# Operands of the second phase from memory, inner P7 in its last block, and the inner weights of P2 formed one phase earlier

## The chip, the cores and the metric

The kernel runs on one core of one Trainium2 chip. The metric is the device time of one execution in microseconds (us), for the kernel before as the median of three runs. A profile is taken of one execution. Its engines are PE (matmuls), DVE and ACT (elementwise work, copies out of PSUM), POOL and SP (which issue most of the DMAs).

## The reference

With one layer of the pooling mixer the computation is, for 4096 frames of width 1024 in float32:

```python
u, gate = jnp.split(rms_norm(x, norm_w) @ in_w, 2, axis=-1)      # 1024 -> 2 x 1024
ug = u.reshape(b, s, POOL_GROUPS, POOL_GROUP_DIM)                # 4 groups of 256
pooled = stack([trailing_mean(ug[:, :, g], w) for g, w in enumerate((2, 4, 8, 16))]) - ug
mixed = jnp.einsum('bsgc,gcd->bsgd', pooled, group_w) + group_b
y = mixed.reshape(b, s, POOL_WIDTH) * scale * jax.nn.silu(gate)
h = x + y @ out_w
return rms_norm(h, final_norm_w)
```

The linear map of each group commutes with the trailing mean, so the kernel folds `group_w` into the left half of `in_w` beforehand and pools afterwards.

## The kernel before

All large products are done by a Strassen-Winograd scheme: a product of 2 x 2 blocks takes seven block products, P1 to P7, of sums and differences of the blocks. Every float32 operand is split into a high part (a copy on ACT, rounded to fp32r) and a low part (a subtraction on DVE), and each block product is three passes of fp32r matmuls (high x high, high x low, low x high). `split(dst, src)` issues the copy and the subtraction.

There are three phases. Phase a is one half of the input projection, phase b the other half, each over four blocks of 1024 frames; phase o is the output projection over eight blocks of 512 frames. Each block is seven steps, one per product: P1, P2, P7, P6, P5, P4, P3 in phases a and b, and P1, P7, P6, P2, P5, P4, P3 in phase o. A plain step of phases a and b is 48 matmuls of 512 columns. In some steps a product is itself done by a further level of the scheme, in seven products of quarter size ("inner" products): P7 of blocks 1 and 2 of phase b (`product_seven`, 84 matmuls of 256 columns, with copies of partial sums from bank to bank on ACT, here called moves), P2 from block 1 of phase o on (`product_inner`, `add_inner`), and an own P7 from block 2 of phase o on. Inner products need inner weights, which are differences of quarters of the plain weights, again split in two.

The names that the rest uses:

- `op0` to `op3` (`op_85` to `op_88` in lists of instructions) are the four buffers of split operands that PE reads; `st` and `vt` are pools of eleven and eight buffers of 512 KB, `w` the split weights, `bank0` to `bank7` (`bank_69` to `bank_76`) the PSUM banks. In lists of instructions each buffer has a number (`st_89` to `st_99` and higher for `st`, `vt_100` to `vt_107` for `vt`).
- `load_in`, `form_in`, `split_in` load, form and split the operands of a step of phases a and b, some steps ahead. In phase a the normalized blocks and one difference are also stored by POOL (`sd`: P1, P2, P7 and P4), phase b loads those and forms the sums for P6, P5 and P3 again.
- `evict_in` copies the banks out after a step: SiLU of the gates after P1 and P2 (into two buffers taken from the pools), and so on. `pool` makes the trailing means of a finished block: for each of its two tiles a short sum, a scan, one scaled difference and two scaled adds on DVE, and then SP stores the tile to `yd` and its buffer goes back to the pool. `pool_due(n)` calls it for what has become due at step n.
- A buffer that comes back to its pool can be taken at once; the instruction that writes it next waits for whatever still reads it, a store included. `take` and `take_v` give out the buffer that has been free longest.
- `load_inner`, `sum_inner`, `split_weight` (L865 and before) load, form and split inner weights in phase o. `load_w(wod, i)`, `form_wb`, `split_wb` bring the output weights in during block 3 of phase b.

The instructions of each engine are put in order by a scheduler when the program is built; `tc.issue_after(x)` holds what is issued inside it behind the instruction x. At run time each engine works its list off in order.

```python
        elif i == P2:
            ev["11"] = [take() for _ in range(2)]
            for c, u in enumerate(cells(ev["11"])):
                last = copy(halved(u), plain(ps[c]), AF.Silu)
```

## Time and profile before

| | |
|---|---|
| median of three runs | 907.35 us (906.75 to 907.79) |
| the profiled execution | 907.23 us |
| its span, first to last instruction | 905.4 us |
| mean granted PE clock | 0.998 |
| PE busy | 895.8 us, 4518 matmuls |
| DVE, ACT, POOL busy | 757.0, 517.5, 118.5 us |
| phase b, blocks 0 to 3 start at about | 323, 396, 468 and 540 us |
| phase o starts at about | 613 us |

In the rows of the profile a line of the timeline gives the start (us), the time from the first start to the last end of the merged instructions, the engine, the line of the kernel, the operation, output<-input by name, the shapes, the count, and in brackets how long the engine had been idle and which work ended that. L79 is the helper through which every instruction of DVE, ACT, POOL and SP is recorded, so these are told apart by names and shapes. L807 are plain products, L753 the inner P7 of phase b, L949 the inner products of phase o, L1681 a few matmuls at the very start. Matmuls are pipelined: a merged row ends some 0.16 us after the next matmul could start.

### The profile page before, as it was taken

The numbers are of one execution on the slowest core, as the hardware profiler recorded it, in microseconds if no ns is written. First come the engines' busy times: TensorE is split into PE (matmuls) and PEld (weight loads), VectorE is DVE, ScalarE is ACT, GpSimd is POOL, SyncE is SP. The second block draws the span as 40 slices with busy tenths as digits, with TensorE's granted clock in tenths as the row PEclk, the third lists the DMA queues.
The fourth block names the chain that finished last, engine by engine and source line by source line (L and its number), as shares of the span: only waits on it lengthen the run. The fifth ranks groups of instructions, "written<-read, shape, count | busy, mean of one in ns | idle before, by whom it ended". The sixth has DMA issues, their size and how long they took to land.

```text
span 905.4 us, 12216 instructions
## 1 busy us (share of the span) xinstructions
PE 895.8 (99%) x4518; PEld 791.1 (87%) x4518; DVE 757.0 (84%) x925; ACT 517.5 (57%) x853; POOL 118.5 (13%) x208
## 2 busy tenths in 40 slices
PE   9999999999999999999999999999999999999996
PEld 7888888888888888889889888888889899999995
DVE  3899995985995999797599499599798878888797
ACT  7869547547445565346545636654657466565464
POOL 0020100100110000000000000001133333343330
PEclk9999999999999999999999999999999999999999
DMA  9987767577675453333554474638483865945953
GB/s 343 401 305 226 273 239 241 187 274 233 235 267 198 164 199 103 99 112 111 202 199 135 179 279 143 197 117 239 143 236 88 212 180 147 233 153 131 259 181 116
DMA packets 71692, 180.49 MB, mean 199 GB/s; under 512 B 6608, under 2 KB 24656, under 8 KB 71632
## 3 DMA queue, kind: packets, MB, share of 16 engines
q1 hardware_dynamic: 54976, 132.50, 42.6%
q0 software_dynamic: 15936, 46.16, 17.6%
q10 hardware_dynamic: 720, 1.06, 0.3%
q8 instruction: 35, 0.57, 0.3%
q14 instruction: 25, 0.20, 0.1%
HBM read 118.86 MB, written 60.83 MB: 198 GB/s over the span
## 4 chain that ended last, share of the span: by engine, by line
PE 87%; DVE 5%; ACT 3%; DMA 2%; issue 2%; POOL 0%; SPq 0%; DVEq 0%; ACTq 0%; POOLq 0%
PE bank L807 78%; PE bank L949 5%; DVE vt L79 2%; PE bank L753 2%; DVE op L79 2%; DMA st<-yd 1%; PE bank L447 1%; DVE st L79 1%; ACT op L79 1%; DMA early<-in_wut 1%; ACT st L79 1%; ACT w L79 0%; ACT vt L79 0%; DMA st<-wod 0%; DVE w L79 0%
## 5 line engine op out<-in xcount | busy, mean ns | idle before, releaser
L807 PE MATMUL bank<-op,w 128*128 128x512 f32 x2592 | 560.9, 379 | 0.1
L807 PEld LDWEIGHTS bank<-op,w 128*128 128x128 f32 x2592 | 489.4, 189 | 70.3 <-ACT vt L79 0.5
L807 PE MATMUL bank<-w,op 128*128 128x512 f32 (+1 forms) x1044 | 230.5, 377 | 0.0
L807 PEld LDWEIGHTS bank<-w,op 128*128 128x128 f32 x1044 | 192.3, 189 | 25.0
L79 DVE TENSOR_TENSOR op<-st,op 128x1024 fp32r<-128x1024 f32 x116 | 141.0, 1222 | 49.7 <-ACT op L79 49.3
L79 ACT ACTIVATE op<-st 128x1024 fp32r<-128x1024 f32 x116 | 121.4, 1051 | 68.7 <-PE bank L807 27.6
L79 ACT ACTIVATE op<-vt 128x1024 fp32r<-128x1024 f32 x67 | 70.4, 1053 | 59.3 <-DVE vt L79 38.7
L79 ACT ACTIVATE vt<-bank 128x512 f32<-128x512 f32 (+1 forms) x124 | 69.6, 580 | 48.0 <-PE bank L807 44.2
L79 DVE TENSOR_TENSOR op<-vt,op 128x1024 fp32r<-128x1024 f32 x67 | 80.9, 1221 | 17.5 <-ACT op L79 17.4
L79 DVE TENSOR_TENSOR st<-st,st 128x1024 f32<-128x1024 f32 (+1 forms) x55 | 63.9, 1181 | 17.6 <-ACT st L79 16.8
L79 POOL DMA_DIRECT2D vt<-in_x x26 | 23.3, 937 | 390.7 <-DVE vt L79 353.8
L79 ACT ACTIVATE bank<-bank 128x512 f32<-128x512 f32 (+1 forms) x78 | 38.7, 498 | 43.5 <-PE bank L807 32.1
L79 DVE TENSOR_TENSOR vt<-bank,vt 128x512 f32<-128x512 f32 (+1 forms) x94 | 54.2, 603 | 7.1 <-PE bank L949 4.6
L79 ACT ACTIVATE st<-bank 128x512 f32<-128x512 f32 (+1 forms) x58 | 33.0, 587 | 31.2 <-PE bank L807 17.4
L79 ACT ACTIVATE st<-st 128x1024 f32<-128x1024 f32 x33 | 34.8, 1056 | 22.6 <-DVE st L79 19.6
L79 DVE TENSOR_TENSOR st<-bank,st 128x512 f32<-128x512 f32 (+1 forms) x68 | 41.2, 625 | 7.4 <-PE bank L807 4.1
L79 DVE TENSOR_TENSOR st<-st,vt 128x1024 f32<-128x1024 f32 (+1 forms) x36 | 41.6, 1175 | 2.2 <-DMA vt<-rd 2.2
L949 PEld LDWEIGHTS bank<-w,op 128*128 128x128 f32 x312 | 40.4, 191 | 1.7
L949 PE MATMUL bank<-w,op 128*128 128x256 f32 x312 | 41.1, 275 | 0.0
L79 DVE TENSOR_TENSOR w<-st,w 128x1024 fp32r<-128x1024 f32 (+1 forms) x27 | 31.6, 1182 | 9.3 <-ACT w L79 9.2
L79 DVE TENSOR_TENSOR_SCAN vt<-vt,window 128x1040 f32<-128x1040 f32 x16 | 38.0, 2381 | 0.3 <-DMA yd<-vt 0.3
L79 DVE TENSOR_TENSOR vt<-vt 128x1024 f32<-128x1024 f32 (+3 forms) x42 | 37.6, 898 | 0.1
(115 smaller groups left out, 720.7 us busy)
## 6 DMA issues: line engine op xcount, KB each, us to landing
st<-in_xt SPq DMA_DIRECT2D x28, 512.0 KB, 6.2
sd<-st POOLq DMA_DIRECT2D x28, 512.0 KB, 4.4
st<-sd SPq DMA_DIRECT2D x26, 512.0 KB, 4.5
st<-in_x SPq DMA_DIRECT2D x21, 512.0 KB, 6.3
yd<-st SPq DMA_DIRECT2D x19, 512.0 KB, 2.9
vt<-yd SPq DMA_DIRECT2D x17, 512.0 KB, 10.4
out<-vt POOLq DMA_DIRECT2D x17, 512.0 KB, 3.3
st<-wod SPq DMA_DIRECT2D x16, 512.0 KB, 4.3
```

The costliest lines, as they stand in the source:

```text
L79: r = f(*args, **kwargs)
L447: latest[0] = nc.tensor.matmul(ps, a[:, kk, 2 * j + t, :], maps, start=t + m == 0, stop=t == 1 and m == len(pairs) - 1,).ins
L753: latest[0] = nc.tensor.matmul(cell(n, c).rearrange("p (a s) -> p a s", s=2), x1, x2, start=i == P1 and k + m == 0, stop=k == 1 and m == 2 ...
L807: latest[0] = nc.tensor.matmul(ps, a, b, start=start and n == 0, stop=stop and n == 2, skip_group_check=True).ins
L949: latest[0] = nc.tensor.matmul(ps, x1, x2, start=start and k + n == 0, stop=k == 1 and n == 2, skip_group_check=True,).ins
```

## The change

It does five things.

1. Phase a stores all seven operands of each block (except P6 of block 0), 22 stores of 512 KB more on POOL. Phase b loads them on SP and no longer forms them on DVE. The history of the pooling (16 columns) is copied in phase b by POOL instead of ACT.
2. P7 of block 3 of phase b is also done as an inner product. The plain P7 weight that was kept for it (`load_plain`, `split_plain`) is gone. `pool_due` is held behind the latest split at P2 of that block.
3. The inner weights of P2 are formed in block 3 of phase b: loaded at P2, summed at P6, split and stored as pairs at P5 and P4, and loaded by POOL in block 0 of phase o. The inner weights of P7 take their place in phase o, all in block 1. The output weights come in five steps (P7 to P3) instead of seven, and their splits stand behind the latest eviction.
4. A difference of weights that phase a saves (`save_t3`) is made in two parts.
5. In the last block of phase o `add_inner` stands ahead of the other evictions of P2, the split of P4's operand behind them, and one normalized row moves from step P2 to step P4.

```diff
@@ sd
-            for i in (P1, P2, P7, P4)
+            for i in range(P1, P7 + 1)
+            if (b, i) != (0, P6)
@@ load_in
+        if q and (b or i not in (P6, P4)):
+            s[operand[i]] = load_saved(b, i)
...
@@ inner_in
-        return q == 1 and 0 < b < NB - 1 and i == P7
+        return q == 1 and b > 0 and i == P7
...
@@ split_in
-        if i == P6 and (q or b):
+        if i == P6 and q == 0 and b:
             form_s4(b)
...
@@ save_inner, take_inner (new)
+        for p in ps:
+            place = next_kept()
+            t = st.keep()
+            home = versions(t)
+            latest_copy[0] = copy(home[0], raws[i][p]).ins
+            latest_split[0] = sub(home[1], raws[i][p], home[0].bitcast(F32)).ins
+            gpsimd.dma_start(out=innerd[p], in_=t)
+            give_kept(place)
...
+                t = st.keep()
+                gpsimd.dma_start(out=t, in_=innerd[p])
+                home = versions(t)
...
@@ pool
+            elif q:
+                gpsimd.tensor_copy(out=v[:, :, 0:HIST], in_=tails[:, g])
             else:
                 copy(v[:, :, 0:HIST], tails[:, g])
@@ evict_o
         if inner and i == P2:
             inner["rows"] = [hs[b][0, j][:, 0] for j in range(2)]
+            if final:
+                add_inner(0, (0, 0))
...
@@ steady, P2 of the last block
-            split(ready[P4], s["22"])
-            give(s.pop("22"))
-            if final:
-                norm_row(b - 1, 0, 1)
+            if not final:
+                split(ready[P4], s["22"])
+                give(s.pop("22"))
             InOrder.on = not final
             product_out(P2, ready.pop(P2), sets, False)
             evict_o(b, P2, sets)
+            if final:
+                split(ready[P4], s["22"])
+                give(s.pop("22"))
...
@@ split_reach
-        if kind == "b" and 0 < b < NB - 1 and i == P6:
+        if kind == "b" and b > 0 and i == P6:
...
@@ forming
-        (0, P4): lambda: load_inner(P2),
-        (0, P3): lambda: sum_inner(P2),
-        (1, P1): lambda: split_weight(P2, P7, P6),
...
+        ("b", NB - 1, P2): lambda: load_inner(P2),
+        ("b", NB - 1, P6): lambda: sum_inner(P2),
+        ("b", NB - 1, P5): lambda: save_inner(P2, P7, P6),
+        ("b", NB - 1, P4): lambda: (save_inner(P2, P4, P5), end_weights(P2)),
+        ("o", 0, P5): lambda: take_inner(P2, P5),
+        ("o", 0, P3): lambda: take_inner(P2, P7, P6, P4),
+        ("o", 1, P7): lambda: load_inner(P7),
...
@@ main loop
-        pool_due(n)
+        with tc.issue_after(latest_split[0]) if (kind, b, i) == ("b", NB - 1, P2) else nullcontext():
+            pool_due(n)
...
             if kind == "b" and b == NB - 1:
-                load_w(wod, i)
+                for p in {P1: (), P2: (), P7: (P1,), P6: (P2, P7), P5: (P6, P5)}.get(i, (i,)):
+                    load_w(wod, p)
```

How the lists of the engines move, at three places. The first is DVE in block 3 of phase b, from step P1 into step P7. Before, a low part of an operand (`op`) stands ahead of each tile of pooling (the scan is the SCALAR_TENSOR_TENSOR row with `window`):

```order
L79 TENSOR_TENSOR op_87<-st_3689,op_87 128x1024
L79 SCALAR_TENSOR_TENSOR st_91<-vt_106,colt,st_91 128x512 x2
L79 SCALAR_TENSOR_TENSOR vt_103<-vt_105,window 128x1040
L79 TENSOR_REDUCE window<-vt_100 128x1
L79 SCALAR_TENSOR_TENSOR vt_103<-vt_103,vt_105 128x2x512
L79 TENSOR_REDUCE window<-vt_104 128x1
L79 SCALAR_TENSOR_TENSOR st_93<-vt_103,colt,st_93 128x512 x2
L79 TENSOR_TENSOR op_88<-vt_107,op_88 128x1024
```

In the changed program, in step P2:

```order
L79 TENSOR_TENSOR op_87<-vt_103,op_87 128x1024
L79 TENSOR_REDUCE window<-vt_107 128x1
L79 TENSOR_REDUCE window<-vt_105 128x1
L79 SCALAR_TENSOR_TENSOR vt_100<-vt_107,window 128x1040
L79 SCALAR_TENSOR_TENSOR vt_104<-vt_105,window 128x1040
L79 SCALAR_TENSOR_TENSOR vt_100<-vt_100,vt_107 128x2x512
L79 SCALAR_TENSOR_TENSOR vt_104<-vt_104,vt_105 128x2x512
L79 SCALAR_TENSOR_TENSOR vt_102<-vt_100,colt,vt_102 128x512 x2
L79 SCALAR_TENSOR_TENSOR st_98<-vt_104,colt,st_98 128x512 x2
L79 TENSOR_TENSOR op_88<-st_94,op_88 128x1024
L79 TENSOR_REDUCE window<-vt_100 128x1
L79 TENSOR_TENSOR op_86<-st_95,op_86 128x1024
```

Both tiles of pooling now stand in one piece between the low part of op_87 and those of op_88 and op_86, and the tile in st_98 is the last of them.

The second place is ACT at the end of step P2 of the same block. Before, with the plain P7 to follow, the four evictions of P2 (the first, second, third and fifth row) have these buffers:

```order
L79 ACTIVATE vt_103<-bank_69 128x512
L79 ACTIVATE vt_103<-bank_70 128x512
L79 ACTIVATE st_92<-bank_71 128x512
L79 ACTIVATE w_1_80<-st_90 128x1024
L79 ACTIVATE st_92<-bank_72 128x512
L79 ACTIVATE op_88<-st_91 128x1024
```

In the changed program, with the inner P7 and its moves (`128x256`) behind them:

```order
L79 ACTIVATE vt_101<-bank_69 128x512
L79 ACTIVATE vt_101<-bank_70 128x512
L79 ACTIVATE op_86<-st_95 128x1024
L79 ACTIVATE st_98<-bank_71 128x512
L79 ACTIVATE st_98<-bank_72 128x512
L79 ACTIVATE bank_71<-bank_69 128x256
L79 ACTIVATE st_95<-bank_69 128x256
L79 ACTIVATE bank_72<-bank_70 128x256
L79 ACTIVATE st_95<-bank_70 128x256
```

The third and fourth evictions now go into st_98, the buffer of the last pooled tile above, and the moves that inner P7 needs stand behind them.

The third place is DVE in the last block of phase o, around step P2; `add_inner` is the row that adds a bank in `128x2x128`. Before:

```order
L79 TENSOR_TENSOR op_87<-vt_102,op_87 128x1024
L79 SCALAR_TENSOR_TENSOR vt_104<-vt_104,ors_0_6674,st_89 128x1024
L79 TENSOR_TENSOR vt_103<-bank_71,vt_103 128x512
L79 TENSOR_TENSOR vt_101<-bank_72,vt_101 128x512
L79 TENSOR_TENSOR vt_103<-bank_69,vt_103 128x2x128
L79 TENSOR_TENSOR op_88<-st_90,op_88 128x1024
```

In the changed program:

```order
L79 TENSOR_TENSOR vt_105<-bank_69,vt_105 128x2x128
L79 TENSOR_TENSOR st_95<-bank_72,st_95 128x512
L79 TENSOR_TENSOR vt_105<-bank_71,vt_105 128x512
L79 TENSOR_TENSOR op_86<-vt_107,op_86 128x1024
L79 TENSOR_TENSOR op_87<-st_4261,op_87 128x1024
```

The first addition from `bank_69` stood behind the low part of an operand, a normalized row (the row with `ors`) and two evictions, and stands ahead of them now.

## The prediction

> **What bounds the kernel now.** I read the page's parts 1 and 4 first, then the timelines of TensorE (PE) where it pauses.

> ```profile
> span 905.4 us, 12216 instructions
> PE 895.8 (99%) x4518; PEld 791.1 (87%) x4518; DVE 757.0 (84%) x925; ACT 517.5 (57%) x853; POOL 118.5 (13%) x208
> PE bank L807 78%; PE bank L949 5%; DVE vt L79 2%; PE bank L753 2%; DVE op L79 2%; DMA st<-yd 1%; PE bank L447 1%; DVE st L79 1%; ACT op L79 1%; DMA early<-in_wut 1%; ACT st L79 1%; ACT w L79 0%; ACT vt L79 0%; DMA st<-wod 0%; DVE w L79 0%
> ```

> PE works for 99% of the span. Time is won only by giving PE less to do or by taking away its few pauses, and work taken from DVE, ACT or a queue counts only where PE waits for it. This is PE around inner P7 of block 1 of phase b, and on to inner P7 of block 2:

> ```profile
> 417.32 2.84 PE L753 MATMUL bank<-op,w 128*128 128x256 f32 x24
> 419.99 0.83 PE L753 MATMUL bank<-op,inner 128*128 128x256 f32 x6
> ...
> 426.92 45.27 PE L807 MATMUL bank<-op,w 128*128 128x512 f32 x209
> 489.08 2.84 PE L753 MATMUL bank<-op,w 128*128 128x256 f32 x24
> ```

> The inner product runs from 417.32 to 426.92, 9.60 us. From there to the next one are six plain products, 62.16 us, 10.36 each. After the start-up PE pauses visibly at three places. The first is the start of P7 in block 3 of phase b:

> ```profile
> 559.98 1.79 PE L807 MATMUL bank<-op,w 128*128 128x512 f32 x6
> 559.47 1.06 ACT L79 ACTIVATE w<-st 128x1024 fp32r<-128x1024 f32 x1 [5.88 <-DMA st<-wod]
> 560.44 1.07 ACT L79 ACTIVATE vt<-bank 128x512 f32<-128x512 f32 x2
> ```

> Six matmuls at 0.216 (10.36 over 48) and a last one of 0.38 are 1.46; the row has 1.79, so 0.33 us is a pause. ACT stood 5.88 us waiting for an output weight, and the evictions behind it were late. The other two are in blocks 1 and 7 of phase o, where an inner product waits for a sum that DVE adds from a bank (`add_inner`):

> ```profile
> 668.12 2.75 PE L807 MATMUL bank<-w,op 128*128 128x512 f32 x12
> 671.19 0.94 PE L949 MATMUL bank<-inner,op 128*128 128x256 f32 x6 [0.31 <-DVE vt L79]
> 880.38 4.05 PE L807 MATMUL bank<-w,op 128*128 128x512 f32 x18
> 885.05 0.94 PE L949 MATMUL bank<-inner,op 128*128 128x256 f32 x6 [0.61 <-DVE vt L79]
> ```

> Twelve matmuls from 668.12 give 670.71, so 0.48 until 671.19, and 0.11 more inside (0.94 against 0.83): 0.58. Eighteen from 880.38 give 884.27: 0.78 and 0.11, 0.87 in the last block.

> **The change part by part.** *Inner P7 in block 3.* PE's own work falls by 10.36 - 9.60 = 0.76 us.

> *The pause at 560.63.* In the changed order no copy of an output weight stands on ACT ahead of these evictions: -0.33.

> *A new wait in the same step.* This term decides the sign. Let T be the start of inner P7 in block 3. At T + 2.67 (419.99 less 417.32) PE writes over its first bank, which ACT must have moved out. In the changed order ACT comes to that move only after two evictions with SiLU into st_98. That buffer has just held a row of the pooling mixer, whose two scaled adds are the last of ten pooling instructions on DVE and which SP then stores to yd. So ACT waits for DVE's ten, for the store to land, and PE waits for ACT. How early can DVE begin? It stands behind the low part of op_87, whose copy ACT can write only when P1 has read its last operand, 10.36 before T. ACT's rows there in block 1, and those of its moves:

> ```profile
> 407.69 0.58 ACT L79 ACTIVATE bank<-bank 128x512 f32<-128x512 f32 x1
> 408.20 1.04 ACT L79 ACTIVATE op<-st 128x1024 fp32r<-128x1024 f32 x1
> ...
> 414.93 0.60 ACT L79 ACTIVATE vt<-bank 128x512 f32<-128x512 f32 x1 [0.70 <-PE bank L807]
> ...
> 418.01 1.05 ACT L79 ACTIVATE op<-st 128x1024 fp32r<-128x1024 f32 x1
> 418.96 0.38 ACT L79 ACTIVATE bank<-bank 128x256 f32<-128x256 f32 x1
> 419.26 0.38 ACT L79 ACTIVATE st<-bank 128x256 f32<-128x256 f32 x1
> ```

> A bank copy and an operand copy take 1.55 (407.69 to 409.24), and I put ACT's start behind PE's last matmul at 0.25, an estimate: op_87's copy is there at T - 10.36 + 1.8 = T - 8.55. Then DVE, whose pooling rows in block 1 are:

> ```profile
> 396.94 2.38 DVE L79 TENSOR_TENSOR_SCAN vt<-vt,window 128x1040 f32<-128x1040 f32 x1 [0.26 <-DMA yd<-vt]
> 399.35 1.23 DVE L79 SCALAR_TENSOR_TENSOR vt<-vt,vt 128x1024 f32<-128x1024 f32 x1
> 400.62 1.42 DVE L79 SCALAR_TENSOR_TENSOR vt<-vt,colt,vt 128x512 f32<-128x512 f32 x2
> 401.95 1.22 DVE L79 TENSOR_TENSOR op<-st,op 128x1024 fp32r<-128x1024 f32 x1
> 403.08 2.38 DVE L79 TENSOR_TENSOR_SCAN vt<-vt,window 128x1040 f32<-128x1040 f32 x1
> ```

> A low part takes 1.13 (401.95 to 403.08): T - 7.4. One tile of pooling takes 5.01 (396.94 to 401.95), and both stand here in one piece: 10.0, so T + 2.6. The four stores of this kind between 530 and 560 us:

> ```profile
> DMA to landing us min/median/max: 2.6/2.6/4.7
> yd<-st SPq DMA_DIRECT2D x19, 512.0 KB, 2.9
> ```

> With 2.9 the buffer is free at T + 5.6 (5.2 with 2.6 and the two scans 0.3 closer, 7.4 with 4.7). ACT then needs about 0.2 to start, 0.98 for two evictions (560.44 again: 1.07 for two, the second 0.49 behind the first), 0.68 for two moves (418.96 to 419.64), and PE 0.1: T + 7.55, that is 4.9 us after T + 2.67. Bounds 4.5 and 6.7. It can't be below nothing, since nothing that ACT or PE does there becomes shorter. I take 4.9, by the median of all 19 stores. While PE waits DVE also finishes the low parts of op_88 and op_86 (T + 5), so no second wait follows.

> *The rest of block 3.* Half-width instructions on DVE follow each other at 0.60:

> ```profile
> 664.05 0.69 DVE L79 TENSOR_TENSOR inner<-st,inner 128x512 fp32r<-128x512 f32 x1
> 664.65 1.22 DVE L79 TENSOR_TENSOR op<-st,op 128x1024 fp32r<-128x1024 f32 x1
> ```

> DVE gets 14 output weights in five steps instead of seven, and four inner ones. Counted in the changed order, from op_87 at P7 to op_85 at P3, DVE has 28 full-width instructions of 1.13, 18 half ones of 0.60, two scans and some small ones, about 50 us, due at T + 61.7. It begins at T + 4, so some 7 us are left, of which waits for weights to land eat a part; the pause itself gives 4.9 more. Cost 0, up to 1.5 if weights land late.

> *Operands from memory.*

> ```profile
> L79 DVE TENSOR_TENSOR st<-st,st 128x1024 f32<-128x1024 f32 x51 | 61.2, 1220 | 17.5 <-ACT st L79 16.8 <-DMA st<-wvd 0.7
> st<-sd SPq DMA_DIRECT2D x26, 512.0 KB, 4.5
> ```

> 22 sums and differences of 1.22 us leave DVE in phase b, all beside PE. The loads that replace them are issued three steps (31 us) ahead and land in 4.5. Phase a gets 22 stores of 512 KB on POOL. Neither ACT nor DVE waits for a store there long enough to reach PE: its waits in the whole trace that the profile can put down are these.

> ```profile
> PE bank L949 <- DVE vt L79: 0.9, 2, 0.6
> PE bank L1681 <- PEq L2014: 0.8, 1, 0.8
> PE bank L447 <- DMA early<-in_wut: 0.5, 1, 0.5
> PE bank L513 <- DVE hl L79: 0.2, 1, 0.2
> ```

> I take 0, with bounds -0.1 and +0.9 (the longest pause of an undisturbed stage).

> *Inner weights of P2.* In block 1 of phase o DVE no longer has four such low parts of inner weights (0.69) before `add_inner`, which was 0.58 late: -0.58, or nothing if the loads by POOL come late.

> *Last block.* `add_inner` goes ahead of the P4 operand and of one normalized row, so the pause of 0.87 goes. But DVE has no idle time from 881.04 to here:

> ```profile
> 881.04 1.22 DVE L79 TENSOR_TENSOR op<-vt,op 128x1024 fp32r<-128x1024 f32 x1
> ...
> 895.20 0.41 DVE L79 SCALAR_TENSOR_TENSOR columns<-columns 128x1 f32<-128x1 f32 x2
> 895.76 0.69 DVE L79 TENSOR_TENSOR vt<-bank,vt 128x512 f32<-128x512 f32 x1
> ```

> Its work only changes places, so it still ends at 895.61, and the last evictions start there instead of at 895.76: -0.15, at most -0.87.

> The sum is -0.76 - 0.33 + 4.9 - 0.58 - 0.15 = +3.1 us. The profiled execution took 907.23, 0.12 under the median of 907.35; on the median this gives 910.4.

> **The rivals.** *The buffer is free in time (faster).* Then -1.8 is left: 905.5. It decides if the store lands by T + 0.7, 4.9 us earlier than worked out; DVE would have to run the pooling ahead of op_87's low part, and the changed order has it behind. For it: DVE has idle time before that instruction. Chance 0.10.

> *The wait is short (within 0.2%).* With less than 3.6 us of wait the rest pays most of it back, 905.6 to 909.1. It takes a P2 step in which DVE is 1.3 us or more ahead, through interleaving that I counted as serial. Chance 0.12.

> *PE restarts slowly (slower still).* The first matmuls of the program, after idle time, are slow:

> ```profile
> 0.78 3.54 PE L1681 MATMUL bank<-const-bfloat16-1.0 128*128 128x512 bf16 x8 [0.78 <-PEq L2014]
> 0.78:4.32 3.54, 3.54 (x8) 1.02 (x8) 0.12 (x2) 1.49 (x2) 0.00 (x0) 1.00 0.65 216
> ```

> 0.44 us each, twice the 0.216 of a 512-column product. If the pause of 4.9 brings that back for the same 3.54 us, half of it is lost, 1.8 more: 912.2. Against it: the granted clock stands at 1.00 even there (the third number from the end), and no pause after the start-up is over 0.8, so nothing here shows a restart. Chance 0.25. [...]

> **How the numbers follow.** The new wait without the slow restart has 0.53 and gives 910.4; its own bounds are 909.9 to 912.4 with the wait alone, and a little under with the phase-o gains larger. With the slow restart it reaches 912.9. The range 908.8 to 912.9 leaves out the faster case and most of the short wait. A measurement of this kernel tells 0.2% (1.8 us) from no change. Slower by more than that: 0.53 + 0.25 = 0.78; within it 0.12; faster 0.10.

> **What would show it.** Right: in block 3 of phase b PE has a pause of 4 to 7 us some 2.7 us into inner P7, ACT's eviction into st there waits for a DMA yd<-st, and DVE runs its pooling scans in the P2 step just before. The three old pauses are gone, inner P7 without the pause takes 9.6. A slow restart would show as matmuls spaced twice as far behind the pause. Wrong: no pause there, or ACT waiting less than 2 us; or a pause elsewhere, in phase a behind a store or in phase o behind an inner weight.

## The result, and the profile after

The changed kernel takes 918.75 us (median of four runs, 917.84 to 920.09) against 907.05 us beside it: a ratio of 1.013 with a 95% interval of 1.0117 to 1.0142. The forecast was 910.4 with a range up to 912.9. The profiled execution took 919.03 us with a span of 917.2, 11.8 more than the span before.

From the page of the changed kernel, the span, the busy times, and the first line of the chain that ended last:

```profile
span 917.2 us, 12432 instructions
PE 898.5 (98%) x4554; PEld 794.6 (87%) x4554; DVE 737.8 (80%) x910; ACT 517.8 (56%) x848; POOL 154.8 (17%) x253
PE 72%; DVE 10%; DMA 7%; issue 6%; ACT 3%; POOL 1%; SPq 0%; DVEq 0%; POOLq 0%; ACTq 0%
```

DVE lost 19 us of work, as the change promised, and the span still grew by 11.8. PE's share of the chain is down from 87% to 72%. PE's waits are listed in the view of waits (line of PE, what it waited for, us in total, times, longest):

```profile
PE bank L745 <- ACT st L79: 4.1, 1, 4.1
PE bank L799 <- DVE op L79: 3.1, 2, 1.9
PE bank L973 <- DVE vt L79: 2.4, 1, 2.4
```

Before, the longest was 0.8. The timeline of PE shows the places (L745 is inner P7 of phase b, L973 the inner products of phase o, L799 plain products):

```profile
560.74 2.84 PE L745 MATMUL bank<-op,w 128*128 128x256 f32 x24
567.68 1.65 PE L745 MATMUL bank<-op,inner 128*128 128x256 f32 x6 [4.10 <-ACT st L79]
569.12 1.49 PE L745 MATMUL bank<-op,w 128*128 128x256 f32 x6
...
577.01 41.61 PE L799 MATMUL bank<-op,w 128*128 128x512 f32 x192
618.45 0.59 PE L799 MATMUL bank<-w,op 128*128 128x512 f32 x2
620.90 10.63 PE L799 MATMUL bank<-w,op 128*128 128x512 f32 x48 [1.85 <-DVE op L79]
632.74 41.27 PE L799 MATMUL bank<-w,op 128*128 128x512 f32 x190 [1.21 <-DVE op L79]
...
677.24 2.76 PE L799 MATMUL bank<-w,op 128*128 128x512 f32 x12
682.42 0.94 PE L973 MATMUL bank<-inner,op 128*128 128x256 f32 x6 [2.42 <-DVE vt L79]
```

Each row gives a term. The inner P7 should go on 2.67 after 560.74 and goes on at 567.68: 4.27 lost. From there to 577.01 are 9.33 us for the matmuls that took 6.93 in block 1 before (419.99 to 426.92): 2.40 lost, with six matmuls of 256 columns in 1.44 (567.68 to 569.12) instead of 0.67. Two matmuls from 618.45 end at 618.88: 2.02 lost before 620.90. The 48 after it give 631.26: 1.48 lost before 632.74. Twelve from 677.24 give 679.83: 2.59 lost before 682.42, and 0.11 inside. That is 12.9. Small pauses in blocks 3 and 5 of phase o add some 0.8 (at 738.88 and 809.92), the gains of the change take off 0.76, 0.33, 0.58 and 0.87, and the end after PE's last matmul is 0.6 longer. Together +11.8.

Behind the first pause stand these rows of DVE, of ACT and of SP's queue:

```profile
552.16 1.23 DVE L79 TENSOR_TENSOR op<-vt,op 128x1024 fp32r<-128x1024 f32 x1 [0.55 <-ACT op L79]
553.49 4.66 DVE L79 TENSOR_TENSOR_SCAN vt<-vt,window 128x1040 f32<-128x1040 f32 x2
558.07 2.34 DVE L79 SCALAR_TENSOR_TENSOR vt<-vt,vt 128x1024 f32<-128x1024 f32 x2
561.64 1.41 DVE L79 SCALAR_TENSOR_TENSOR st<-vt,colt,st 128x512 f32<-128x512 f32 x2
563.08 0.32 SPq L79 DMA_DIRECT2D yd<-st  x1
565.97 1.08 ACT L79 ACTIVATE st<-bank 128x512 f32<-128x512 f32 x2 [3.90 <-DMA yd<-st]
```

The low part of op_87, then both tiles of pooling in one piece, the store, and ACT's eviction 3.90 us idle until that store has landed: the chain of the prediction, row for row. The pauses at the start of phase o have another cause:

```profile
609.97 1.23 DVE L79 TENSOR_TENSOR w<-st,w 128x1024 fp32r<-128x1024 f32 x1 [1.61 <-ACT w L79]
613.82 1.23 DVE L79 TENSOR_TENSOR w<-st,w 128x1024 fp32r<-128x1024 f32 x1 [2.02 <-ACT w L79]
617.36 2.35 DVE L79 TENSOR_TENSOR w<-st,w 128x1024 fp32r<-128x1024 f32 x2
619.63 1.22 DVE L79 TENSOR_TENSOR op<-st,op 128x1024 fp32r<-128x1024 f32 x1
```

The low part of an operand that PE needs at 618.88 starts at 619.63, behind four low parts of output weights. DVE stood still twice for such a weight (3.63 us), because ACT's copy of it waited for its load: in the view of the `st` tiles between 596 and 618 us the engines' idle time is put down mostly to these loads.

```profile
  DMA st<-wod: 8.8, 4
DMA to landing us min/median/max: 3.4/4.5/6.9
```

The third pause begins on POOL, which now issues the loads of inner weights:

```profile
651.49 0.91 POOL L79 DMA_DIRECT2D w<-inner  x1 [4.33 <-PE bank L799]
658.71 0.91 POOL L79 DMA_DIRECT2D w<-inner  x1 [6.31 <-issue]
660.60 0.71 POOL L79 TENSOR_TENSOR oss<-parts 128x2 f32<-128x2 f32 x1
```

POOL got to its second load 6.31 us after it had issued the first, with no wait that the profile shows, and the small normalizing operation `oss`, on which ACT and DVE wait, stood behind it. Before, this operation started 17.7 us ahead of the block's first inner product (647.08 to 664.78); here 13.2 (660.60 to 673.85). In the variants of the changed kernel below the pause follows this lead: 13.2 and 13.5 us of lead (here and in run 1) go with 2.59 and 2.35 us of pause, 15.3 and 15.4 (runs 2 and 4) with 1.08 and 0.95, 16.9 and 18.2 (runs 3 and 9) with none.

### The profile page after: what moved, and what is told of

It is laid out like the page before. It is cut to its first block, busy times and chain, and to the rows that moved or that the text cites. A ratio compares the mean times of both kernels' runs of the same rounds, so it can differ in the third digit from the quotient of the medians.

```text
span 917.2 us, 12432 instructions
## 1 busy us (share of the span) xinstructions
PE 898.5 (98%) x4554; PEld 794.6 (87%) x4554; DVE 737.8 (80%) x910; ACT 517.8 (56%) x848; POOL 154.8 (17%) x253
## 3 DMA queue, kind: packets, MB, share of 16 engines
q10 hardware_dynamic: 720, 1.06, 0.3%
## 4 chain that ended last, share of the span: by engine, by line
PE 72%; DVE 10%; DMA 7%; issue 6%; ACT 3%; POOL 1%; SPq 0%; DVEq 0%; POOLq 0%; ACTq 0%
PE bank L799 65%; DVE vt L79 4%; PE bank L745 3%; PE bank L973 3%; DVE op L79 3%; DMA vt<-yd 2%; DVE st L79 2%; DMA st<-wod 2%; PE bank L451 1%; DVE w L79 1%; DMA st<-in_x 1%; DMA early<-in_wut 1%; DMA out<-vt 1%; ACT w L79 1%; ACT st L79 1%
## 5 line engine op out<-in xcount | busy, mean ns | idle before, releaser
L799 PE MATMUL bank<-op,w 128*128 128x512 f32 x2544 | 550.5, 379 | 0.0
L799 PEld LDWEIGHTS bank<-op,w 128*128 128x128 f32 x2544 | 480.4, 189 | 68.6 <-ACT bank L79 0.4
L799 PE MATMUL bank<-w,op 128*128 128x512 f32 (+1 forms) x1044 | 231.0, 377 | 3.1 <-DVE op L79 3.1
L799 PEld LDWEIGHTS bank<-w,op 128*128 128x128 f32 x1044 | 192.1, 189 | 28.7 <-DVE op L79 3.9
L79 DVE TENSOR_TENSOR op<-st,op 128x1024 fp32r<-128x1024 f32 x120 | 146.1, 1221 | 67.2 <-ACT op L79 66.9
L79 ACT ACTIVATE op<-st 128x1024 fp32r<-128x1024 f32 x120 | 125.9, 1052 | 92.1 <-DVE st L79 37.7
L79 ACT ACTIVATE op<-vt 128x1024 fp32r<-128x1024 f32 x65 | 68.4, 1054 | 73.8 <-DVE vt L79 43.1
L79 DVE TENSOR_TENSOR op<-vt,op 128x1024 fp32r<-128x1024 f32 x65 | 78.5, 1220 | 14.5 <-ACT op L79 14.5
L79 ACT ACTIVATE vt<-bank 128x512 f32<-128x512 f32 (+1 forms) x120 | 66.2, 575 | 42.0 <-PE bank L799 34.4
L79 DVE TENSOR_TENSOR st<-st,st 128x1024 f32<-128x1024 f32 (+1 forms) x45 | 49.4, 1113 | 29.7 <-ACT st L79 16.8
L79 ACT ACTIVATE bank<-bank 128x512 f32<-128x512 f32 (+1 forms) x84 | 41.1, 490 | 44.3 <-PE bank L799 31.1
L79 POOL COPY vt<-tails 128x32 f32<-128x32 f32 x14 | 17.5, 1258 | 274.7 <-ACT tails L79 101.1
L79 ACT ACTIVATE st<-bank 128x512 f32<-128x512 f32 (+1 forms) x64 | 36.4, 589 | 33.6 <-PE bank L799 15.6
L79 DVE TENSOR_TENSOR vt<-bank,vt 128x512 f32<-128x512 f32 (+1 forms) x80 | 47.4, 617 | 5.8 <-PE bank L973 4.5
L79 DVE TENSOR_TENSOR st<-bank,st 128x512 f32<-128x512 f32 (+1 forms) x82 | 47.7, 602 | 5.1 <-DMA st<-in_x 4.0
L79 ACT ACTIVATE st<-st 128x1024 f32<-128x1024 f32 x34 | 35.8, 1056 | 26.4 <-DVE st L79 24.9
L79 POOL DMA_DIRECT2D sd<-st x45 | 24.1, 536 | 124.9 <-DVE st L79 77.4
L79 DVE TENSOR_TENSOR st<-st,vt 128x1024 f32<-128x1024 f32 (+1 forms) x36 | 41.6, 1172 | 2.8 <-DMA vt<-rd 2.8
L973 PEld LDWEIGHTS bank<-w,op 128*128 128x128 f32 x312 | 40.3, 191 | 2.7 <-ACT bank L79 1.1
L973 PE MATMUL bank<-w,op 128*128 128x256 f32 x312 | 41.4, 276 | 0.3 <-ACT bank L79 0.2
L79 DVE TENSOR_TENSOR_SCAN vt<-vt,window 128x1040 f32<-128x1040 f32 x16 | 37.8, 2376 | 0.7 <-DMA wod<-vt 0.6
L79 DVE TENSOR_TENSOR vt<-vt 128x1024 f32<-128x1024 f32 (+3 forms) x42 | 38.1, 909 | 0.2
## 6 DMA issues: line engine op xcount, KB each, us to landing
sd<-st POOLq DMA_DIRECT2D x45, 512.0 KB, 4.5
st<-sd SPq DMA_DIRECT2D x42, 512.0 KB, 3.7
st<-in_xt SPq DMA_DIRECT2D x28, 512.0 KB, 7.4
st<-in_x SPq DMA_DIRECT2D x22, 512.0 KB, 7.4
yd<-st SPq DMA_DIRECT2D x21, 512.0 KB, 3.7
vt<-yd SPq DMA_DIRECT2D x18, 512.0 KB, 10.9
out<-vt POOLq DMA_DIRECT2D x16, 512.0 KB, 3.2
st<-wod SPq DMA_DIRECT2D x15, 512.0 KB, 5.3
```

What stands on the lines that cost most here:

```text
L79: r = f(*args, **kwargs)
L799: latest[0] = nc.tensor.matmul(ps, a, b, start=start and n == 0, stop=stop and n == 2, skip_group_check=True).ins
L973: latest[0] = nc.tensor.matmul(ps, x1, x2, start=start and k + n == 0, stop=k == 1 and n == 2, skip_group_check=True,).ins
```

## The experiments

**1. Pooling not held.**

```diff
-        with tc.issue_after(latest_split[0]) if (kind, b, i) == ("b", NB - 1, P2) else nullcontext():
-            pool_due(n)
+        pool_due(n)
```

> The changed kernel without the hold of the pooling behind the latest split at P2 of block 3 of phase b; nothing else is edited. The wait of 4.3 us in inner P7 there, and the slow matmuls behind it (2.4 us lost), should go if both come from the order of DVE. Theory A (the two late low parts at the start of phase o, 3.6 us, are DVE's own lateness and the pause gave DVE time): the pause goes, but the DVE weights come later still, so that the pauses at the start of phase o grow from 3.6 us to about 6 to 8; about 915 us. Theory B (those two pauses are weight loads that land late, and PE's position does not matter to them): 6.7 us are won, 912 us. If the slow matmuls have nothing to do with the pause, 4.3 us at most are won and inner P7 still takes 12 us without a pause.

913.44 us, ratio to before 1.0063 (1.0047 to 1.0080). The slow matmuls went with the pause: 565.43 to 572.46 is 7.03.

```profile
561.96 2.84 PE L745 MATMUL bank<-op,w 128*128 128x256 f32 x24
565.43 0.94 PE L745 MATMUL bank<-op,inner 128*128 128x256 f32 x6 [0.63 <-ACT st L79]
572.46 41.61 PE L799 MATMUL bank<-op,w 128*128 128x512 f32 x192
...
617.90 10.63 PE L799 MATMUL bank<-w,op 128*128 128x512 f32 x48 [3.41 <-DVE op L79]
629.52 41.27 PE L799 MATMUL bank<-w,op 128*128 128x512 f32 x190 [0.99 <-DVE op L79]
```

The pauses at the start of phase o grew from 3.50 to 4.83 (613.90 plus 0.43 to 617.90 is 3.57, and 617.90 plus 10.36 to 629.52 is 1.26), and PE had a new one of 1.3 us ahead of P7, waiting for an eviction. The time lies between the two theories. That the long pause had covered for DVE is not shown: in run 3, which has no such pause either, the two at the start of phase o are 0.52 and 2.2 us.

**2. Inner weights loaded by SP.**

```diff
-                gpsimd.dma_start(out=t, in_=innerd[p])
+                sync.dma_start(out=t.bitcast(F32), in_=innerd[p].bitcast(F32))
```

and the same for the two halves of the weight for P5.

> The changed kernel with the four kinds of inner-weight loads of block 0 of phase o issued by SP instead of POOL. Theory A (POOL waits behind its own load in small pieces, the small normalizing operations that POOL does for block 1 are late, DVE waits for them, and the sum from a bank for inner P2 comes 2.6 us late): the pause at 679.6 us falls to 0.2 us or nothing, 2.4 us less, about 916.3 us. Theory B (the pause is DVE's own load in that block, which no longer has the slack): the pause stays above 2 us and the time is 918.7 us. Theory C (SP's queue has the output rows to load, and the small pieces now hold those up): a new pause in block 1 or 2 of phase o, the time within 1 us of 918.7 or above it.

915.88 us, 1.0092 (1.0074 to 1.0110). The pause in block 1 of phase o fell from 2.59 to 1.08 us and no new one came, though the two at the start of phase o are 0.8 us longer together in this profile (4.27). So theory A for 1.5 us of the 2.4 that it forecast; where the rest comes from is not shown.

**3. Both.**

> Both edits together: pooling not held at P2 of block 3, inner weights loaded by SP. If the two causes are independent the savings add up: about 909.5 to 912.5 us (918.7 less 6.7 or 4, less 2.4). What is left above the kernel before is then the two pauses at the start of phase o. If DVE's lateness there has merely been covered by the pause, these pauses are longer than 3.6 us together in this profile.

912.10 us, 1.0045 (1.0031 to 1.0059), as expected, and the pause in block 1 of phase o is gone altogether. One thing was not expected: a pause of 2.2 us at the start of phase o was followed by slow matmuls (the granted clock is 0.50 from 627.96 to 631.38), while one of 3.57 us in run 1 was not (1.00 from 608 to 624). That is taken up below.

**4. Both, and output weights in seven steps.**

```diff
-                for p in {P1: (), P2: (), P7: (P1,), P6: (P2, P7), P5: (P6, P5)}.get(i, (i,)):
-                    load_w(wod, p)
+                load_w(wod, i)
```

> The two edits, and the output weights loaded in seven steps as in the kernel before instead of five. Theory A (the two late low parts at the start of phase o come from the output weights being asked for one and two steps late, through one buffer, so that DVE waits for landings of 5.4 to 6.9 us): these pauses go too, 3.6 us more, and the gains of the change are left alone, 0.76 + 0.33 + 0.58 + 0.87: 905 to 906.5 us, faster than before. Theory B (DVE has too much work in block 3 of phase b with four inner weights more, whenever they are loaded): the pauses at the start of phase o stay, 909 to 912 us. A short wait in inner P7 of block 3, of up to 1.7 us, can come with the earlier loads.

907.51 us, 1.0000 (0.9990 to 1.0009): 4.6 us less than run 3. The pauses at the start of phase o are gone altogether (613.47 to the first inner product without one), so they came from weights that were asked for late, theory A. The splits of these weights moved forward with the loads, and this run does not tell the two apart. The time is 1 us above that theory's range. Left are 1.6 us in inner P7 of block 3 and 0.95 in block 1 of phase o. In P7 the moves stand on ACT behind two copies of the output weight of P2 (the row of two `w`):

```profile
561.44 1.05 ACT L79 ACTIVATE op<-st 128x1024 fp32r<-128x1024 f32 x1
562.38 1.99 ACT L79 ACTIVATE w<-vt 128x1024 fp32r<-128x1024 f32 x2
564.28 0.37 ACT L79 ACTIVATE bank<-bank 128x256 f32<-128x256 f32 x1
```

**5. Pauses made on purpose.** A number of times the same low part is subtracted again, in the kernel before:

```diff
+            for _ in range(0 if h else again):
+                latest_split[0] = sub(t[:, 1], u, t[:, 0].bitcast(F32)).ins
```

> The kernel before, where the low part of one operand is subtracted again 5, 5, 10, 12 and 6 times, each time with the same result (1.13 us each on DVE), at P4 of block 0, P6 of block 1, P7 of block 2 and P7 of block 3 of phase a, and at P1 of block 0 of phase b. Each makes PE pause once, by what the low part's lead there does not cover: by the rows of before about 3.2, 2.5, 3.7, 5.5 and 4.6 us (near 86, 138, 200, 272 and 324 us; where the scheduler moves other work, some tenths to a few us more or less). Nothing else changes there: no inner product, no move, no store. Theory A (PE's clock falls in a pause of some length between 2.4 and 4.1 us): behind the longest pauses the matmuls are spaced twice as far for a few us, the granted clock of that stretch is under 0.9, and behind the shortest they are not; which pauses have it tells the length. Theory B (the slow matmuls of the changed kernel come from what else happens in inner P7: moves, traffic, small matmuls): no pause here is followed by slow matmuls, and each costs its own length only.

960.42 us in one run. The pauses came out longer than I had worked out, since other instructions of DVE and ACT were pushed along (4.5, 7.0, 2.8, 6.6, 4.1 and 9.3 us were the largest). Behind each group of them the matmuls of 512 columns stood about 0.43 apart instead of 0.216 (in the 4.50 us from 153.50 PE was busy throughout, on 11 of them, at a granted clock of 0.50). The clock does fall in a pause, as in theory A, but the length alone does not decide: 2.2 us were followed by a fall in run 3, 3.57 in run 1 were not. These are windows of 1 us around the moments at which the granted clock changed (it is the third number from the end):

```profile
90.00:91.00 1.00, 0.71 (x1) 0.26 (x1) 1.00 (x2) 0.00 (x0) 0.00 (x0) 0.67 0.96 315
151.00:152.00 1.00, 0.00 (x0) 0.00 (x0) 1.00 (x2) 0.98 (x2) 0.00 (x0) 0.88 0.98 164
158.00:159.00 1.00, 1.00 (x5) 0.85 (x4) 0.00 (x0) 0.00 (x0) 0.00 (x0) 0.70 0.46 185
223.00:224.00 1.00, 0.00 (x0) 0.00 (x0) 1.00 (x2) 0.00 (x0) 0.00 (x0) 0.72 0.97 377
301.00:302.00 1.00, 0.00 (x0) 0.00 (x0) 1.00 (x2) 0.00 (x0) 0.00 (x0) 0.98 0.87 178
315.00:316.00 1.00, 1.00 (x5) 0.85 (x4) 1.00 (x2) 0.00 (x0) 0.00 (x0) 0.70 0.00 0
370.00:371.00 1.00, 0.00 (x0) 0.00 (x0) 1.00 (x2) 0.00 (x0) 0.00 (x0) 0.61 0.00 0
```

In these traces the granted clock has two values, 1.00 and 0.50. So 0.67 over 90 to 91 means full for 0.34 us and then half: it fell at 90.34. In the same way it fell at 151.76, 223.44, 301.96 and 370.22, and came back at 158.60 and 315.60. The five falls are 61.42, 71.68, 78.52 and 68.26 apart. These distances differ from each other by 3.42 (71.68 less 68.26) or a multiple of it, and are 18, 21, 23 and 20 times 3.413 (279.88 in all, over 82 steps). The two returns are 6.84 and 13.64 after their falls, 2 and 4 times that. So all seven changes lie on one grid of 3.413 us, which in this execution did not move with the pauses.

**6. Inner P7 alone, in the kernel before.**

```diff
-        return q == 1 and 0 < b < NB - 1 and i == P7
+        return q == 1 and b > 0 and i == P7
```

with the same in `split_reach`, the inner weights kept to block 3 and the plain weight no longer loaded.

> The kernel before with one part of the change alone: P7 of block 3 of phase b as an inner product, its plain weight no longer kept; pooling not held, operands formed as before, inner weights of P2 as before. Theory A (an inner P7 fits into this block, and the hold of the pooling is the whole cause of the wait): 906 to 907 us. Theory B (this block has no room for it unless DVE is relieved, since the output weights' splits stand between the evictions and the moves): a pause in inner P7 there, longer than the 4.3 us of the changed kernel, and 914 to 920 us; then the stored operands are what the inner P7 needs, and the hold is a loss inside a plan that otherwise works.

916.89 us, 1.0102 (1.0086 to 1.0117): theory B. Inner P7 lost 7.4 us in three waits, the longest with the loads of output weights between ACT's moves:

```profile
564.90 0.40 ACT L79 ACTIVATE bank<-bank 128x256 f32<-128x256 f32 x1
568.56 1.06 ACT L79 ACTIVATE w<-st 128x1024 fp32r<-128x1024 f32 x1 [3.26 <-DMA st<-wod]
570.91 0.38 ACT L79 ACTIVATE st<-bank 128x256 f32<-128x256 f32 x1 [1.29 <-DVE w L79]
```

**7 and 11. Stored operands alone, and with the difference of weights in two parts.** The edits are the hunks of the change on `sd`, `load_in`, `form_in`, `split_in` and `pool`; run 11 adds those on `save_t3`.

> The kernel before with another part alone: all operands of phase a stored, those of phase b loaded, the history copied by POOL; plain P7 and everything behind it as before. The prediction's term for it was nothing (-0.1 to +0.9 us). Right: 906.8 to 908.3 us, no pause in phases a and b of over 0.5 us that before has not. Rival (22 more stores of 512 KB on POOL's queue and 26 more loads on SP's hold up the loads of x, or POOL's copies of the history are late): a pause in phase a or b, 908.5 us or more.

913.75 us, 1.0067 (1.0053 to 1.0080): a pause in phase a as in the rival, and my term was wrong for this part by itself. The cause is another than the rival's: ACT's evictions waited for a subtraction of two weights on DVE (the difference that `save_t3` makes), and that for its load. ACT and PE around the place:

```profile
223.74 2.07 ACT L79 ACTIVATE st<-bank 128x512 f32<-128x512 f32 x4 [6.92 <-DVE st L79]
224.39 15.93 PE L807 MATMUL bank<-op,w 128*128 128x512 f32 x65 [3.48 <-ACT st L79]
```

> All operands stored and loaded, as in the run of that part alone, with the difference of weights that phase a saves made in two parts as in the changed kernel. In the run of that part alone PE paused 3.6 us at 220.5 us: ACT's evictions waited 6.9 us for a subtraction on DVE of two weights, whose load was issued late, behind the first half's store, and took 5.4 us under the heavier traffic. Theory A (one buffer is loaded, subtracted, stored and loaded again within one step): with two steps for it the pause and the slow matmuls behind it go, 5.3 us, 908 to 908.5 us. Theory B (the traffic itself delays the loads): the pause stays above 2 us, 912 us or more.

906.59 us, 0.9997 (0.9988 to 1.0007): theory A, all of the loss is gone, and the time is 1.4 us under the range expected. Stores and loads together cost nothing that can be measured, once the difference has two steps.

**8. Output weights loaded in between.** P1 in step P1, P2 in P7, P7 and P6 in P6, the rest each in its step.

> The changed kernel with pooling not held, inner weights loaded by SP, and the output weights loaded nearly as before (P1 in step P1, P2 in step P7, P7 and P6 in step P6, the rest each in its step), so that no copies of weights of P2 stand on ACT ahead of the moves of inner P7 in block 3. In the version with seven steps PE waited there 1.4 us. If those copies are the cause: under 0.8 us there, about 906.5 us. If it is the store of the pooled tile, as in the changed kernel: 1.4 us again and 907.5. The two pauses at the start of phase o must stay away, as with seven steps; if they come back the loads are still too late, 909 or more.

914.47 us, 1.0076 (1.0062 to 1.0089): a miss. P7 had three waits instead of one (about 2.8 us together), for an eviction, a low part and a move; phase o had one of 2.1 us on ACT at 625.6, and 1.8 in block 1. Loading the weights of P2 and P7 one step later than in run 4 moved the trouble on and did not remove it. I did not follow each of these waits to its origin.

**9. Loaded in seven steps, but the weights of P2 split one step later.**

```diff
-                load_w(wod, i)
+                if i == P2:
+                    held = []
+                    for h in range(2):
+                        held.append(take())
+                        sync.dma_start(out=held[-1], in_=wod[P2][h])
+                else:
+                    if i == P7:
+                        for h, u in enumerate(held):
+                            with tc.issue_after(evicted[0]):
+                                split(w[P2][h], u)
+                            give(u)
+                    load_w(wod, i)
```

> The changed kernel with pooling not held, inner weights loaded by SP and output weights loaded in seven steps, and the output weights of P2 split one step later than they are loaded, behind inner P7, so that no copy of them stands on ACT ahead of its moves. The version with the early split waited there 1.4 us and took 907.5 us. If the copies are the cause of that wait: 0.3 us or less, 906.0 to 906.5 us, under the kernel before by 0.1% or more. If the evictions wait for a buffer anyway: 1 us or more again and 907.5. The pause before the sum from a bank in block 1 of phase o (0.9 us) stays in both cases.

905.56 us, 0.9986 (0.9977 to 0.9996): 1.4% faster than the changed kernel, and faster than the kernel before by 0.14%, with an interval that just leaves out no change. The pause in block 1 of phase o, which was expected to stay, went too. PE's waits after the start-up have gone from the list, and inner P7 of block 3 runs as in blocks 1 and 2:

```profile
560.71 2.84 PE L745 MATMUL bank<-op,w 128*128 128x256 f32 x24
563.39 0.83 PE L745 MATMUL bank<-op,inner 128*128 128x256 f32 x6
...
570.32 41.61 PE L799 MATMUL bank<-op,w 128*128 128x512 f32 x192
```

PE's last matmul ends 2.5 us earlier than before (895.92 against 898.40), which is 0.76 + 0.33 + 0.58 + 0.87. Of this 0.8 goes again, since the end behind it takes 7.8 us instead of 7.0.

**10. The last block alone, in the kernel before.**

> The kernel before with the reordering of the last block alone (sum from a bank first, the split of P4's operand behind the evictions, one normalized row from step P2 to step P4). The prediction's term: the pause of 0.87 us in the last block goes, and as DVE is busy throughout and ends when it did, 0.15 us is won, at most 0.87. Rival: DVE loses by the new order, the last evictions come up to 1 us later against PE's end, and the time from PE's last matmul to the end of the span grows from 7.0 to 7.8 us, so that nothing or a loss of up to 0.2 us is left. Between 906.5 and 907.6 us either way; the profile tells them apart.

907.02 us, 0.9998 (0.9989 to 1.0007). PE ended 0.7 earlier, and the rest after it took 8.1 us instead of 7.0: the rival. The time by itself does not tell it from the prediction's 0.15.

## Why the prediction was wrong

The sign and the first mechanism were right; three us became twelve. The steps that failed are three terms of the sum: the slow restart, left out of it (measured 2.40 us), "the rest of block 3", put at 0 (3.50), and the inner weights of P2, put at -0.58 (+2.1). In the profiles they make 8.6 of the 8.7 us by which the sum was too small. What is left misses by less than 1 us each time and nearly cancels.

*"A new wait in the same step", 4.9 us.* Right: 4.27, by the chain that was worked out, with the store at 2.8 (the `yd<-st` of 563.08 landed at 565.88). Run 1 takes the hold away: 0.80 of the 4.27 stay in this place, and 1.3 come new ahead of P7.

*"PE restarts slowly", put at 0.25 and 1.8 us.* It happened, and cost 2.40. The step that failed was the evidence against it: "no pause after the start-up is over 0.8, so nothing here shows a restart" speaks of pauses that were too short to show anything. The other evidence, the granted clock of 1.00 beside the slow first matmuls, said nothing either. The trace of the kernel before has no entry of the clock ahead of 4.16 us, that of the changed kernel none ahead of 5.92, and the column prints 1.00 where there is none. In the changed kernel 3 matmuls of 256 columns fall into 1.2 us ahead of that moment and 7 into 1.2 us behind it, both beside a 1.00:

```profile
4.70:5.90 1.20, 1.20 (x3) 1.02 (x4) 0.00 (x0) 0.39 (x1) 0.00 (x0) 1.00 0.78 289
6.00:7.20 1.20, 1.20 (x7) 1.06 (x6) 0.60 (x1) 0.75 (x3) 0.00 (x0) 1.00 0.91 309
```

Behind the first pause the clock falls while PE stands still and returns 6.84 us later:

```profile
565.00:566.00 1.00, 0.00 (x0) 0.00 (x0) 0.56 (x2) 0.03 (x1) 0.46 (x1) 0.85 1.16 205
572.00:573.00 1.00, 1.00 (x9) 1.00 (x9) 0.93 (x1) 0.04 (x1) 0.00 (x0) 0.73 0.26 37
```

That is 565.70 and 572.54, two of the steps of run 5 apart. PE worked in 4.86 us of that, at half speed: 2.4 us lost. Of the 3.41 us before the fall 2.28 were idle here (PE stopped at 563.42), in run 3 2.17 (625.79 to 627.96), and in run 5 2.06 before the fall at 301.96 (from 299.90). The largest idle share of a step that had no consequence in the changed kernel's profile is 1.90 of 3.41 (679.84 to 681.74, which is 34 steps behind 565.70). My estimate from these four is that the idle time within one step decides, with the bound between 1.90 and 2.06 us of 3.41 (56% and 60%). A pause of 3.57 us as in run 1 can then escape if it is split between two steps, and by the grid it was. The clock of run 1 falls only behind the last matmul, at 909.68, and that places its grid (in the changed kernel, too, the fall behind the last matmul, at 913.86, is on the grid: 348.16 us behind 565.70, 102 steps of 3.4133):

```profile
909.00:910.00 1.00, 0.00 (x0) 0.00 (x0) 0.00 (x0) 0.00 (x0) 0.00 (x0) 0.84 0.60 207
```

86 steps of 3.4133 us earlier is 616.14, which cuts the pause (614.33 to 617.90) into 1.81 and 1.76 us, each under the 1.90 that had no consequence.

*"The rest of block 3 … Cost 0, up to 1.5 if weights land late."* It cost 3.5, and the step from run 3 to run 4 takes it away by asking for the weights earlier, without less work for DVE. I counted DVE's work (50 us in 58) and took 7 us of slack; waits for weights ate it. Two weights in one step make a chain of load, copy, low part, and DVE's wait for a landing of up to 6.9 us stands in its queue ahead of the operands.

*"Inner weights of P2 … -0.58 … or nothing if the loads by POOL come late."* It came to +2.1 (2.59 and 0.11 lost, where 0.58 was lost before). The loads were in time (the last landed at 664.6, the inner products begin at 673.85); what stood behind them was POOL's own work. I priced the loads for the one who waits for them and not for what stands behind them at the engine that issues them. Run 2 moved them and took 1.5 of the 2.6 us away.

*"Operands from memory", 0.* Right in the sum (run 11), but only since the change also splits `save_t3`; alone it loses 6.5 us (run 7), of which 3.6 are a pause and 1.7 the half clock behind it. My prediction passed over that hunk.

*"Last block", -0.15.* The time can't tell (run 10), but the reason is not borne out: the last evictions start at 896.11 there and not at 895.61. (The pause before is 0.78 and 0.11, which is 0.89 and not 0.87.)

## What to carry to other kernels

A change that only saves work can lose a per cent through the order in which the rest is queued; price every instruction that moves by what stands behind it on its own engine, loads on the engine that issues them included. Where PE never waits, a new wait of a few us can cost more than its own length, as the 4.27 us here cost 2.40 more: count the matmuls that run at half clock after it (the clock came back 3.42 us after its fall in run 3, 6.84 here, 6.84 and 13.64 in run 5). And when a change loses, repair its order piece by piece before dropping it: with four small edits (runs 1, 2, 4 and 9) the same change is 0.14% faster than the kernel before, where it was 1.3% slower.
